# Attention tiles in shared rings, packed transposed weights, a larger landing reserve and a 128-row g_pre in a hybrid streaming encoder layer

## The chip, the cores and the metric

The kernel runs on one NeuronCore of a Trainium2 chip, on its five engines: TensorE (PE) multiplies, VectorE (DVE), ScalarE (ACT) and GpSimd (POOL) do the elementwise work, SyncE (SP) issues the DMAs. The metric is the device time of one execution in microseconds, and the lower the better.

## What is computed

One layer for a prompt of 1024 tokens and a later chunk of 32 tokens that share the weights; D = 1024, eight heads of 64 in each of two attention groups, float32 throughout. The reference, cut to what matters:

```python
def in_proj(h, g_pre, w_in):
    u = rmsnorm(h, g_pre) @ w_in                      # 1024 -> 4096
    qa, ka, va, ga, qb, kb, vb, gb = jnp.split(u, SPLIT_IDX, axis=-1)
def band_attention(q, k, v, q_pos, k_pos, bias_table):      # group A: softmax, own chunk and 8 before
    s = jnp.einsum('bqhd,bkhd->bhqk', q, k) * ATTN_SCALE + bias_table[:, rel][None]
    w = jax.nn.softmax(jnp.where(ok[None, None], s, NEG_INF), axis=-1)
    return jnp.einsum('bhqk,bkhd->bqhd', w, v)
def stick_breaking(q, k, v, q_pos, k_pos):                  # group B: strictly causal
    z = jnp.einsum('bqhd,bkhd->bhqk', q, k) * ATTN_SCALE
    log_beta = jax.nn.log_sigmoid(z)
    log_1m = jnp.where(causal, jax.nn.log_sigmoid(-z), 0.0)
    after = lax.cumsum(log_1m, axis=3, reverse=True) - log_1m
    w = jnp.where(causal, jnp.exp(log_beta + after), 0.0)
    return jnp.einsum('bhqk,bkhd->bqhd', w, v)
def finish(h, oa, ga, ob, gb, w_out, g_post, p, w_ple, w_ple_gate):
    y = jnp.concatenate([oa * jax.nn.silu(ga), ob * jax.nn.silu(gb)], axis=-1) @ w_out
    h = h + rmsnorm(y, g_post)
    return h + jax.nn.sigmoid(h @ w_ple_gate) * (p @ w_ple)
```

The sample chunk attends over a cache of 512 tokens and itself. New keys and values are outputs too.

## The kernel before

Every float32 product is made from two rounded parts: x = hi + lo, and PE adds hi*hi, hi*lo and lo*hi. So each operand is cast to hi by ACT or POOL, and lo = x - hi is made by DVE or POOL.

The work has three stages. **The start** loads x in nine tiles of 128 tokens (`load_x`, tiles x0 to x8, x3 and x4 in the tile x34), squares them on ACT (`scale_x`, tile sq), scales them with the row factor rs and with g_pre, transposes them on PE (`turn_x`, ptx) and keeps them as hnh and hnl in three chunks of 352 tokens. g_pre is spread to all partitions by a product of a column of ones with the row ghl (gpre). Beside this, half of p @ w_ple is made (tiles wph, wpl, php; results ple). Twelve matmuls on zeros (idle) stand ahead of everything on PE.

**The attention** takes eight pairs of heads, A0, B0, A1, B1 and so on to B3. `col_steps` projects a pair's k, q and v (mm_kA, mm_qA, mm_vA, 24 matmuls of 352 columns for each of three chunks); the weights of the next projection are loaded as wr and split into wh and wl (`ensure`). Keys and values go out, and the values are brought to token order through DRAM: DVE transposes 32x32 blocks (vx), a DMA writes swapA or swapB, four DMAs read it back into st (`values_out`), ACT copies it to vt, and `prep_v` splits it into v2. `prep_k` makes kd and kl with two copying DMAs, `prep_q` makes L.

For each head and each block i of 128 queries, `attention` has three steps. `scores(i)` makes S in PSUM from L, kd and kl, and the weights in two SBUF tiles of 1024 columns: w0 (named om) and w1 (named be). Group A adds the bias and takes the maximum on DVE, the exponential on ACT, the scaling by 1/sum on POOL. Group B takes two sigmoids on ACT, a scan on DVE and a product on POOL. `weights_t(i)` transposes w1 by blocks on PE into PSUM (ptw), and ACT and DVE evict it as hi and lo into wTh and wTl. `values(g)` multiplies four query blocks at once with v2 into PSUM (PV), 24 matmuls a head. om and be have three buffers each, wTh and wTl two each, of 4 x 512 columns: one for each group of four key blocks. The sample's heads run through the same tiles (`sample_attention`); its new values wait in vsT until then.

Projections of the next pair are woven between the attention steps as filling work for PE, and the gate projections (mm_gA, mm_gB) between and behind the last. Beside this POOL subtracts blocks of w_out and w_ple_gate (oB, gB) for the third stage.

**The finish** makes the output projection and the gate as seven block products in place of eight (o0P to g3P), and everything behind.

What sets the order of the instructions is a planner (`Recorder.order`, line 307). All steps are recorded first, each with its engine, an estimated duration and what it depends on. The planner then plays the program through: each engine takes, of what is ready at its time, the step with the lowest key, attention ahead of projections on PE. The result is written out as it stands, so each engine works strictly in that order. For a DMA it reckons the time at which it has landed:

```python
                line = max(line, t + o.busy + DMA_NS) + o.late
                done = line + DMA_MARGIN
```

DMA_NS is 1500 and DMA_MARGIN 800 (line 165). A tile's buffer comes free for the planner when the last use of the tile that held it has been placed. All instructions of the program are issued at line 385, so the profile names that line for all of them, and tiles tell them apart.

Of the kernel before, what the change touches and what calls it, by code (L numbers as in the profile page):

```python
# [13 lines left out]
P = 128  # L14
# [12 lines left out]
NT = 9  # L27

# [127 lines left out]

class Op:
# [7 lines left out]
DMA_NS, DMA_RATE, DMA_MARGIN = 1500, 320.0, 800  # L165
# [3 lines left out]
class Pool:  # L169
# [8 lines left out]
    def tile(self, shape, dtype, tag=None, name=None, bufs=1):  # L178
# [7 lines left out]
        line.append(b)  # L186
        return b
# [12 lines left out]
class Recorder:  # L200
# [43 lines left out]
    def add(self, eng, what, args, kw):  # L244
        writes, reads = [], []
        method = what[1] if isinstance(what, tuple) else ""
        for i, a in enumerate(args):
            if isinstance(a, (View, Raw)):
                (writes if i == 0 or (method == "tensor_tensor_reduce" and i == 7) else reads).append(a)
        for k, a in kw.items():  # L250
            if isinstance(a, (View, Raw)):
                (writes if k in ("out", "accum_out") else reads).append(a)
# [16 lines left out]
        if eng == "DVE":  # L269
            sbuf = [v for v in reads if isinstance(v, View) and not v.buf.psum and v.free() > 4]  # L270
# [3 lines left out]
    def cost(eng, method, args, kw, writes, reads):  # L274
# [3 lines left out]
        psum = any(isinstance(v, View) and v.buf.psum for v in reads)  # L278
# [96 lines left out]
    def emit(self, tc):  # L375
        ops = self.order()
        with tc.manual_schedule():
            for o in ops:
# [3 lines left out]
                args = [a.get() if isinstance(a, (View, Raw)) else a for a in o.args]  # L382
                kw = {k: a.get() if isinstance(a, (View, Raw)) else a for k, a in o.kw.items()}
# [7 lines left out]
def stream_step(  # L391
# [26 lines left out]
    r_dr = scratch([8, 768], "r_dr")  # L418
    ple_dr = scratch([T, D], "ple_dr")
# [55 lines left out]
    def ensure(j):  # L475
# [6 lines left out]
        if j == 2:  # L482
            pair = [at.tile([P, 2, 4, P], F32R, tag=tag, name=f"{tag}_{kind}{p}", bufs=2) for tag in ("wTh", "wTl")]
# [14 lines left out]
    def load_x(t):  # L498
        n = min(P, T - t * P)
        if t == 3:  # L500
            x34.append(at.tile([P, 2, D], F32, tag="wTh", name="x34", bufs=2))
        xt = x34[0][:, t - 3] if t in (3, 4) else at.tile([P, D], F32, tag="om", name=f"x{t}", bufs=3)
# [9 lines left out]
    def scale_x(t, xt, n, gp):  # L512
        sq = at.tile([P, D], F32, tag="be", name=f"sq{t}", bufs=3)
# [25 lines left out]
    def bias_rows():  # L539

        rb = at.tile([8, 257], F32, tag="om", name="rb", bufs=3)
        dma(rb, rel_bias[0])
        R = at.tile([8, 768], F32, tag="be", name="R", bufs=3)
# [101 lines left out]
    def col_steps(j):  # L645
# [65 lines left out]
    def attention(ab, p, h):  # L711
# [16 lines left out]
        def scores(i):  # L728
# [5 lines left out]
            w0 = at.tile([P, SEQ + 1], F32, tag="om", name=f"om{nm}_{i}", bufs=3)  # L734
            w1 = at.tile([P, SEQ], F32, tag="be", name=f"be{nm}_{i}", bufs=3)
# [31 lines left out]
            state[i] = w1  # L767

        wT = {}

        def weights_t(i):
            g, q = i // 4, (i % 4) * P
            for j in range(i // 4 + 1):
                if (g, j) not in wT:
                    wT[g, j] = [at.tile([P, 4, 4 * P], F32R, tag=tag, name=f"{tag}{nm}_{g}_{j}", bufs=2) for tag in ("wTh", "wTl")]
            b0 = lo_block(i)
            w1 = state.pop(i)
            b = b0
            while b <= i:
                j = b // 4  # L780
                e = min(i + 1, 4 * (j + 1))
                m = e - b
                pt = psum("T", f"ptw{nm}_{i}_{j}")
                for x in range(m):
                    nc.tensor.transpose(pt[:, x * P:(x + 1) * P], w1[:, (b - b0 + x) * P:(b - b0 + x + 1) * P], ident)
                hi, lo = wT[g, j]
                o = b - 4 * j
                src = pt[:, 0:m * P].rearrange("p (b c) -> p b c", b=m)
                nc.scalar.copy(hi[:, o:o + m, q:q + P], src)
                nc.vector.tensor_tensor(lo[:, o:o + m, q:q + P], src, f(hi[:, o:o + m, q:q + P]), ALU.subtract)  # L790
                b = e
# [946 lines left out]
```

## Time and profile before

| | |
|---|---|
| time, median of three runs | 824.11 us (823.62 to 825.51) |
| the profiled execution, its own time | 822.94 us |
| its span, first to last instruction | 821.2 us |
| PE busy | 806.5 us, 98% |
| DVE, ACT, POOL busy | 588.7, 536.5, 498.6 us |
| mean granted PE clock | 0.999 |
| DMA | 135.57 MB in 137855 packets |

A page of the profile and the views of its trace tell of one execution. Matmuls are pipelined and their ends are modelled, so the mean duration of a matmul holds the overlap with the next; the distance from one start to the next tells what a matmul costs. In a row of the timeline stand the start, the length that the instructions of the row cover together, the engine, the operation with out<-in, the count, and in brackets the idle time of the engine ahead of it with what ended it. In the list of waits a row names who waited for whom, the total in microseconds, how often, and the longest.

### The profile page before, as it was taken

Reading aid. Unit: us, or ns where it says so; the run is one execution under the profiler, and the core shown is the slowest. Engines: PE = TensorE matmul, PEld = TensorE weight load, DVE = VectorE, ACT = ScalarE, POOL = GpSimd, SP = SyncE. Lnnn points to the kernel's source line nnn. Section 1 sums busy time; section 2 is a strip of 40 time slices with the busy share of each in tenths; the row PEclk is TensorE's granted clock in tenths of the full one; section 3 lists DMA queues with packets and bytes.
Section 4 is the critical chain, followed back from the end, with each engine's and each line's share of the span. In section 5 each row is a group of like instructions: output and inputs, shape, how many; then the busy total and the mean of one; then the engine's idle time right before and its main releaser. Section 6 shows DMA issues by size and latency. Waiting matters only on the chain.

```text
span 821.2 us, 14722 instructions
## 1 busy us (share of the span) xinstructions
PE 806.5 (98%) x4814; PEld 742.7 (90%) x4814; DVE 588.7 (72%) x1165; ACT 536.5 (65%) x1179; POOL 498.6 (61%) x559
## 2 busy tenths in 40 slices
PE   9999999999999999999999999999999999999997
PEld 7999999999999998999999998999998787888786
DVE  5717588987687898687887787983664676686755
ACT  4735588776476667687685676653437866886741
POOL 5625785996676959554753454675462527599613
PEclk9999999999999999999999999999999999999999
DMA  8419854526764545633413544253489847749733
GB/s 296 122 39 277 208 178 149 142 60 203 214 178 155 152 135 153 154 91 88 97 40 98 139 122 145 74 160 112 134 264 291 293 142 242 252 153 361 248 117 128
DMA packets 137855, 135.57 MB, mean 165 GB/s; under 512 B 36450, under 2 KB 103818, under 8 KB 137779
## 3 DMA queue, kind: packets, MB, share of 16 engines
q1 hardware_dynamic: 137778, 134.64, 55.0%
q8 instruction: 38, 0.62, 0.3%
q14 instruction: 39, 0.31, 0.2%
HBM read 85.41 MB, written 40.79 MB: 154 GB/s over the span
## 4 chain that ended last, share of the span: by engine, by line
PE 83%; DVE 6%; ACT 4%; DMA 4%; issue 2%; SPq 0%; POOL 0%; DVEq 0%; ACTq 0%
PE mm_gB L385 5%; PE mm_qA L385 5%; PE mm_kB L385 5%; PE mm_kA L385 5%; PE mm_vA L385 4%; PE mm_vB L385 4%; PE mm_qB L385 4%; PE PVB L385 4%; PE SB L385 3%; PE ple L385 3%; PE PVA L385 3%; PE mm_gA L385 3%; PE ptwB L385 3%; PE ptwA L385 3%; PE SA L385 3%; PE g1P L385 2%
## 5 line engine op out<-in xcount | busy, mean ns | idle before, releaser
L385 POOL TENSOR_TENSOR beB<-beB,omB 128x128 f32<-128x128 f32 (+7 forms) x64 | 87.2, 1364 | 75.3 <-ACT beB L385 31.5
L385 DVE TENSOR_TENSOR_SCAN omB<-omB 128x128 f32<-128x128 f32 (+7 forms) x64 | 106.5, 1675 | 6.6 <-POOL omB L385 3.5
L385 POOL TENSOR_SCALAR beA<-beA,statA 128x640 f32<-128x640 f32 (+2 forms) x64 | 48.2, 755 | 50.1 <-DVE statA L385 47.9
L385 DVE TENSOR_TENSOR wTlA<-ptwA,wThA 128x128 fp32r<-128x128 f32 (+3 forms) x96 | 45.5, 483 | 27.8 <-ACT wThA L385 27.0
L385 ACT CAST wThA<-ptwA 128x128 fp32r<-128x128 f32 (+3 forms) x96 | 39.7, 422 | 32.1 <-PE ptwA L385 30.5
L385 ACT ACTIVATE omB<-SB 128x384 f32<-128x384 f32 (+5 forms) x96 | 47.1, 501 | 14.7 <-DVE SB L385 8.3
L385 DVE TENSOR_TENSOR wTlB<-ptwB,wThB 128x512 fp32r<-128x512 f32 (+3 forms) x96 | 50.7, 545 | 8.1 <-ACT wThB L385 7.2
L385 ACT CAST wThB<-ptwB 128x512 fp32r<-128x512 f32 (+3 forms) x96 | 44.7, 485 | 16.9 <-PE ptwB L385 16.3
L385 ACT ACTIVATE beA<-omA,statA 128x640 f32<-128x640 f32 (+2 forms) x64 | 44.7, 700 | 7.2 <-DVE statA L385 5.6
L385 ACT ACTIVATE beB<-SB 128x384 f32<-128x384 f32 (+5 forms) x96 | 45.4, 500 | 6.0 <-PE ptwB L385 3.2
L385 PE MATMUL ptwB<-ident,beB 128*128 128x128 f32 x288 | 44.9, 274 | 0.1
L385 PE MATMUL ptwA<-ident,beA 128*128 128x128 f32 x240 | 40.2, 274 | 0.8 <-POOL beA L385 0.8
L385 PEld LDWEIGHTS ptwB<-ident,beB 128*128 128x128 f32 x288 | 34.9, 140 | 3.4 <-DVE wTlB L385 0.8
L385 POOL TENSOR_TENSOR gB<-gB,gB 128x256 f32<-128x256 f32 x32 | 29.1, 929 | 13.8 <-issue 7.4
L385 PE MATMUL SB<-kdB,LB 128*128 128x384 f32 (+5 forms) x96 | 34.6, 364 | 0.3 <-ACT beB L385 0.2
L385 POOL TENSOR_TENSOR oB<-oB,oB 128x256 f32<-128x256 f32 x32 | 28.4, 903 | 8.6 <-DMA oB<-in_w_out_dram 4.6
L385 PE MATMUL SB<-klB,LB 128*128 128x384 f32 (+5 forms) x96 | 33.1, 346 | 0.0
L385 DVE CUSTOM_DVE_ANT_0 omA<-SA,biasA 128x320 f32<-128x320 f32 (+2 forms) x64 | 30.7, 479 | 3.2 <-PE SA L385 1.9
L385 PEld LDWEIGHTS ptwA<-ident,beA 128*128 128x128 f32 x240 | 30.2, 140 | 2.7 <-POOL beA L385 1.1
L385 PE MATMUL SA<-kdA,LA 128*128 128x320 f32 (+2 forms) x96 | 30.5, 327 | 1.4 <-DVE LA L385 1.2
L385 PE MATMUL SA<-klA,LA 128*128 128x320 f32 (+2 forms) x96 | 29.9, 321 | 0.0
L385 POOL TENSOR_TENSOR h<-h,x 128x512 f32<-128x512 f32 (+1 forms) x18 | 23.3, 1321 | 0.8 <-DVE h L385 0.8
(712 smaller groups left out, 2674.5 us busy)
## 6 DMA issues: line engine op xcount, KB each, us to landing
x<-in_x_prompt_dram SPq DMA_DIRECT2D x8, 512.0 KB, 5.9
oB<-in_w_out_dram SPq DMA_DIRECT2D x16, 256.0 KB, 4.0
sum_dro<-oB SPq DMA_DIRECT2D x16, 256.0 KB, 2.3
gB<-in_w_ple_gate_dram SPq DMA_DIRECT2D x16, 256.0 KB, 3.8
sum_drg<-gB SPq DMA_DIRECT2D x16, 256.0 KB, 2.8
x<-in_x_prompt_dram SPq DMA_DIRECT2D x16, 256.0 KB, 3.7
h_dr<-h SPq DMA_DIRECT2D x8, 512.0 KB, 3.5
ht<-h_dr SPq DMA_DIRECT2D x8, 512.0 KB, 5.5
```

The source lines that it names most:

```text
L385: getattr(getattr(tc.nc, o.what[0]), o.what[1])(*args, **kw)
```

## The change

It has five parts.

1. om and be are no longer buffers of 1024 columns but stretches of one long tile each (`Arena`): 3076 columns for om, 3384 for be. A tile takes the columns that it needs, one behind the other, and starts again at 0 where the rest is too short. It depends on the earlier tiles with which its columns overlap. All tiles that lived in om and be (x, sq, the bias rows, the sample's caches Kc and Vc) take their stretch there. In the changed kernel's order all of them are called om or be.
2. wTh and wTl become two such rings of 33 blocks of 128 columns. A group of four query blocks takes 13 or 20 blocks in A, 13 or 29 in B (`LAID`): the blocks of one query block lie side by side, and each query block starts 3, 4 or 7 blocks behind the one before. `weights_t` transposes four blocks at a time from the first on, and evicts them into one run; before, the cuts lay at multiples of four key blocks. `values` reads its moving operand as runs of 128 columns with a fixed step (`Segments`).
3. DMA_MARGIN goes from 800 to 2000.
4. g_pre: ones and ghl have 128 rows in place of one. Rows 1 to 127 of ghl are set to zero by two memsets on DVE.
5. The sample's new values go to DRAM (vs_dr) by a DMA for each pair, and come back into one tile vn for four heads; the POOL copies into vsT go.

The function `swapped` returns False for everything, so the branch behind it is never recorded. The diff, cut to its core:

```diff
-DMA_NS, DMA_RATE, DMA_MARGIN = 1500, 320.0, 800
+DMA_NS, DMA_RATE, DMA_MARGIN = 1500, 320.0, 2000
+class Segments:
+    def __init__(self, buf, start, step, n):
+        self.buf, self.start, self.step, self.n = buf, start, step, n
+        self.shape = [buf.shape[0], n, P]
+        self.box = (buf.box[0], (start, start + (n - 1) * step + P))
+    def get(self):
+        base = self.buf.get()[:, self.start:self.start + P]
+        return bass.AP(tensor=base.tensor, offset=base.offset, ap=[base.ap[0], [self.step, self.n], [1, P]])
+class Arena:
+    def tile(self, shape, name, dtype=None):
...
+        size = -(-n // 8) * 8
+        if self.at + size > self.cols:
+            self.at = 0
+        lo, hi = self.at, self.at + size
+        self.at = hi
...
+        for c, d, x in self.live:
+            if c < hi and lo < d:
+                old.append(x)
+                left += [(p, q, x) for p, q in ((c, lo), (hi, d)) if p < q]
+            else:
+                left.append((c, d, x))
...
-    vsT = const.tile([NS, 4, P], F32, tag="vsT", name="vsT")
+    ring0, ring1 = Arena(rec, at, "om", 3076), Arena(rec, at, "be", 3384)
+    ringh, ringl = (Arena(rec, at, x, 33 * P, F32R) for x in ("wTh", "wTl"))
...
-            nc.gpsimd.tensor_scalar(vsT[:, slot(ab, p), :], tok[0:NS, 8, :], 1.0, 1.0, ALU.mult, ALU.mult)
+            dma(vs_dr[ab][:, p * P:(p + 1) * P], tok[0:NS, 8, :])
...
-            w0 = at.tile([P, SEQ + 1], F32, tag="om", name=f"om{nm}_{i}", bufs=3)
-            w1 = at.tile([P, SEQ], F32, tag="be", name=f"be{nm}_{i}", bufs=3)
+            w0 = ring0.tile([P, n + (ab == "B")], f"om{nm}_{i}")
+            w1 = ring1.tile([P, n], f"be{nm}_{i}")
...
+        LAID = {("A", 0): (3, 13), ("A", 1): (4, 20), ("B", 0): (3, 13), ("B", 1): (7, 29)}
         def weights_t(i):
...
-                nc.scalar.copy(hi[:, o:o + m, q:q + P], src)
-                nc.vector.tensor_tensor(lo[:, o:o + m, q:q + P], src, f(hi[:, o:o + m, q:q + P]), ALU.subtract)
+            for b in range(0, n, 4):
+                m = min(4, n - b)
+                pt = psum("T", f"ptw{nm}_{i}_{b}")
                 for x in range(m):
+                    nc.tensor.transpose(pt[:, x * P:(x + 1) * P], w1[:, (b + x) * P:(b + x + 1) * P], ident)
+                c = slice(b * P, (b + m) * P)
+                nc.scalar.copy(hi[:, c], pt[:, 0:m * P])
+                nc.vector.tensor_tensor(lo[:, c], pt[:, 0:m * P], f(hi[:, c]), ALU.subtract)
...
-                nc.tensor.matmul(acc[:, c], v2[:, b, :], wT[g, j][half][:, b - 4 * j, c], start=(n == 0), stop=(n == len(todo) - 1))
+                step = LAID[ab, g][0]
+                w = Segments(wT[g][half], c.start * step + b * P, step * P, (c.stop - c.start) // P)
+                nc.tensor.matmul(acc[:, c], v2[:, b, :], w, start=(n == 0), stop=(n == len(todo) - 1))
...
+            vn = at.tile([NS, 256], F32, tag="ot", name="vn" + nm, bufs=3)
+            dma(vn, vs_dr[ab][:, 256 * gi:256 * gi + 256])
...
-    ones = at.tile([1, P], F32R, tag="ot", name="ones", bufs=3)
+    ones = at.tile([P, P], F32R, tag="ot", name="ones", bufs=3)
     nc.gpsimd.memset(f(ones), 1.0)
-    ghl = at.tile([1, 2, D], F32R, tag="wTl", name="ghl", bufs=2)
+    ghl = ringl.tile([P, 2, D], "ghl")
+    for part in range(2):
+        nc.vector.memset(f(ghl[:, part]), 0.0)
```

**What moves, at three places.** The first is PE's order just ahead of the first values product of pair B3 (PVB30), which waits for v2B30; SB30 are scores of the same head, ptksB1 a transpose for the sample, mm_gA0 the gate projection that fills. Before:

```order
L385 MATMUL ptksB10_6937<-ident_111,KcsB1_6841 128x128 x4
L385 MATMUL mm_gA0_1_6780<-hnh1_106,wl_gA0_1_6504 128x352
L385 MATMUL mm_gA0_1_6780<-hnl1_109,wh_gA0_0_6535 128x352 x2
L385 MATMUL ptksB11_6952<-ident_111,KcsB1_6841 128x128 x4
L385 MATMUL mm_gA0_1_6780<-hnl1_109,wh_gA0_0_6535 128x352 x2
L385 MATMUL mm_gA0_1_6780<-hnl1_109,wh_gA0_1_6566 128x352 x4
L385 MATMUL mm_gA0_2_6915<-hnh2_107,wh_gA0_0_6535 128x352 x3
L385 MATMUL PVB30_0_6872<-wThB30_0_0_6805,v2B30_6408 128x512
```

Now, in the same place:

```order
L453 MATMUL SB30_7_0_6602<-kdB30_5743,LB30_5749 128x512
L453 MATMUL SB30_7_0_6602<-klB30_5748,LB30_5749 128x512
L453 MATMUL mm_gA0_1_6452<-hnh1_108,wl_gA0_1_6169 128x352 x4
L453 MATMUL mm_gA0_1_6452<-hnl1_111,wh_gA0_0_6184 128x352 x2
L453 MATMUL SB30_7_1_6619<-kdB30_5743,LB30_5749 128x512
L453 MATMUL SB30_7_1_6619<-klB30_5748,LB30_5749 128x512
L453 MATMUL mm_gA0_1_6452<-hnl1_111,wh_gA0_0_6184 128x352 x2
L453 MATMUL ptwB30_4_0_6628<-ident_113,be_147 128x128 x4
L453 MATMUL mm_gA0_1_6452<-hnl1_111,wh_gA0_1_6239 128x352 x4
L453 MATMUL mm_gA0_2_6570<-hnh2_109,wh_gA0_0_6184 128x352 x4
L453 MATMUL mm_gA0_2_6570<-hnh2_109,wh_gA0_1_6239 128x352 x3
L453 MATMUL PVB30_0_6522<-wTh_493,v2B30_6096 128x512
```

The scores of block 7 and the transposes of block 4 have moved ahead of this product, and the gate projections follow behind them.

The second is ACT's order around the casts of pair B1's value weights (wh_vB1, which wait for the DMA into wr_vB1), in head A10. Before:

```order
L385 CAST wThA10_1_1_2800<-ptwA10_6_1_2930 128x3x128
L385 CAST wThA10_1_0_2522<-ptwA10_7_0_2931 128x128
L385 CAST wh_vB1_0_2778<-wr_vB1_0_2909 128x512
L385 ACTIVATE stqB1_2478<-mm_qB1_1_2807 128x352
L385 CAST wh_vB1_1_2785<-wr_vB1_1_2910 128x512
L385 CAST wThA10_1_1_2800<-ptwA10_7_1_2982 128x4x128
```

Now:

```order
L453 ACTIVATE stqB1_2296<-mm_qB1_1_2718 128x352
L453 CAST wTh_493<-ptwA10_6_4_2825 128x128
L453 ACTIVATE be_147,statA11_2_2544<-om_133,statA11_2_2544 128x384
L453 CAST wTh_493<-ptwA10_7_0_2826 128x512
L453 CAST wh_vB1_0_2697<-wr_vB1_0_2782 128x512
L453 CAST wh_vB1_1_2709<-wr_vB1_1_2783 128x512
L453 CAST wTh_493<-ptwA10_7_4_2858 128x128
```

A projection's eviction and an exponential now stand ahead of the two casts, and of the transposed weights one block stands behind them, before four.

The third is POOL's order in head A01: the rows be with stat are the scalings that the transposes on PE wait for, oB the differences of w_out blocks that wait for loads. Before:

```order
L385 TENSOR_SCALAR beA01_0_1228<-beA01_0_1228,statA01_0_994 128x128
L385 TENSOR_TENSOR oB110_974<-oB220_973,oB110_974 128x256
L385 TENSOR_TENSOR oB210_1235<-oB110_974,oB210_1235 128x256 x2
L385 TENSOR_SCALAR beA01_1_1315<-beA01_1_1315,statA01_1_1012 128x256
L385 TENSOR_TENSOR wl_kA1_0_1307<-wr_kA1_0_865,wh_kA1_0_1328 128x512
```

Now:

```order
L453 TENSOR_SCALAR be_147<-be_147,statA01_0_974 128x128
L453 TENSOR_SCALAR be_147<-be_147,statA01_1_987 128x256
L453 TENSOR_TENSOR oB120_922<-oB120_922,oB110_924 128x256 x2
L453 TENSOR_TENSOR oB110_924<-oB220_923,oB110_924 128x256
L453 TENSOR_SCALAR be_147<-be_147,statA01_2_1007 128x384
```

The scaling of block 1 has moved ahead of the differences, and the differences come later in the head.

More of the change, by code (lines that the diff above doesn't have):

```diff
@@ L27, with swapped @@
 NT = 9
+def swapped(ab, p, h, i):
+    return False
 LAG_T = 2
@@ L277, in cost @@
         n = out.free() if isinstance(out, View) else 1
-        psum = any(isinstance(v, View) and v.buf.psum for v in reads)
+        psum = any(isinstance(v, (View, Segments)) and v.buf.psum for v in reads)
         if eng == "PE":
@@ L482, in ensure @@
         if j == 2:
-            pair = [at.tile([P, 2, 4, P], F32R, tag=tag, name=f"{tag}_{kind}{p}", bufs=2) for tag in ("wTh", "wTl")]
+            pair = [ringl.tile([P, 2, 4, P], f"w{x}_{kind}{p}") for x in "hl"]
         for kh in range(2):
@@ L766, in scores @@
                 nc.gpsimd.tensor_scalar(w1[:, 0:n], w1[:, 0:n], m[:, 3:4], 1.0, ALU.mult, ALU.mult)
-            state[i] = w1
+            state[i] = w0, w1
         wT = {}
+        LAID = {("A", 0): (3, 13), ("A", 1): (4, 20), ("B", 0): (3, 13), ("B", 1): (7, 29)}
         def weights_t(i):
[L772 to L775, printed above, removed]
+            g = i // 4
+            step, size = LAID[ab, g]
+            if g not in wT:
+                wT[g] = [x.tile([P, size * P], f"{x.name}{nm}_{g}") for x in (ringh, ringl)]
```

97 lines of the change are left out of this document (64 added, 33 removed).

## The prediction, made before the changed kernel had run

> **What bounds the kernel now.** I read the page first: the shares of the engines and the chain that ended last.
>
> ```profile
> PE 806.5 (98%) x4814; PEld 742.7 (90%) x4814; DVE 588.7 (72%) x1165; ACT 536.5 (65%) x1179; POOL 498.6 (61%) x559
> PE 83%; DVE 6%; ACT 4%; DMA 4%; issue 2%; SPq 0%; POOL 0%; DVEq 0%; ACTq 0%
> ```
>
> TensorE (PE) is the bound, and the change leaves it the same 4814 matmuls of the same widths. So a gain can only come from PE standing idle or running slowly. The table of busy time by stretches tells where it stands idle; the columns are the stretch, its length, then the busy time of each engine.
>
> ```profile
> 20.00:25.00 5.00, 4.32 (x28) 3.62 (x27) 3.25 (x7) 4.36 (x12) 4.59 (x8) 1.00 0.96 316
> 40.00:62.00 22.00, 22.00 (x142) 21.38 (x141) 4.13 (x9) 7.34 (x15) 4.79 (x9) 1.00 0.16 42
> 62.00:130.00 68.00, 65.32 (x426) 62.84 (x425) 47.90 (x131) 46.51 (x108) 47.09 (x60) 1.00 0.75 202
> 200.00:270.00 70.00, 68.19 (x451) 65.74 (x450) 51.68 (x132) 47.05 (x111) 46.70 (x63) 1.00 0.64 184
> 480.00:545.00 65.00, 62.94 (x405) 59.84 (x404) 54.87 (x85) 44.74 (x99) 40.55 (x43) 1.00 0.48 139
> 780.00:821.20 41.20, 36.43 (x169) 29.96 (x168) 21.58 (x35) 13.26 (x23) 10.31 (x8) 0.98 0.38 122
> ```
>
> Of 14.7 us idle, 4.8 are the tail, which the change leaves alone, and 6.6 lie in three stretches of the attention (2.7, 1.8 and 2.1). The waits of PE name them:
>
> ```profile
> PE PVB L385 <- DVE v2B L385: 1.8, 1, 1.8
> PE PVA L385 <- ACT wThA L385: 1.2, 1, 1.2
> PE SA L385 <- DVE LA L385: 1.2, 1, 1.2
> PE ptwA L385 <- POOL beA L385: 0.8, 1, 0.8
> PE PVA L385 <- DVE v2A L385: 0.6, 1, 0.6
> PE ptksB L385 <- DVE v2B L385: 0.5, 1, 0.5
> ```
>
> All but the third go back to a DMA that landed later than the order had reckoned. The timeline shows the engine that stood before such a landing, with its idle time and releaser in brackets:
>
> ```profile
> 510.21 1.05 ACT L385 COPY vtB<-stvB 128x1024 f32<-128x1024 f32 x1 [2.95 <-DMA stvB<-swapB]
> 221.71 0.62 ACT L385 CAST wh_vB<-wr_vB 128x512 fp32r<-128x512 f32 x1 [2.90 <-DMA wr_vB<-in_w_in_dram]
> 105.67 0.73 POOL L385 TENSOR_TENSOR oB<-oB,oB 128x256 f32<-128x256 f32 x1 [2.05 <-DMA oB<-in_w_out_dram]
> ```
>
> ACT waits for the swapped values at 510, and the values product waits behind it (1.8 us). At 221 it waits for raw weights, with the last cast of the transposed weights queued behind (1.2). At 105 POOL waits for w_out, with a softmax scaling queued behind (0.8). Together 4.9 us of PE time hang on landings.
>
> The other slow place is the start, PE's timeline:
>
> ```profile
> 1.31 2.93 PE L385 MATMUL idle<-newh 128*128 128x256 f32 x12 [1.31 <-DVE newh L385]
> 4.05 1.94 PE L385 MATMUL ptp<-ident,pp 128*128 128x128 f32 x8
> 5.92 2.07 PE L385 MATMUL gpre<-ghl,ones 1*128 1x512 f32 x4
> 7.92 3.78 PE L385 MATMUL ple<-wph0True,php 128*128 128x512 f32 x8
> 11.50 1.91 PE L385 MATMUL ple<-wpl0True,php 128*128 128x512 f32 x4
> 13.21 2.37 PE L385 MATMUL ple<-wph1True,php 128*128 128x512 f32 x8
> 15.42 0.60 PE L385 MATMUL ptx<-ident,sq 128*128 128x128 f32 x4
> 34.68 3.90 PE mm_vA L385 x24
> 625.11 5.57 PE ple L385 x24
> ```
>
> The last two rows, from the chain, give full speed: 162 ns for 352 columns, 232 ns for 512. From 11.50 to 13.21 four 512-column matmuls took 427 ns each: half speed. The next eight took 2.21 us, which is two at 427 and six at 232, so the speed doubled near 14.0 us, 6.1 us after the first matmul with 128 rows of real data (7.92). The granted clock reads 1.00 all this time, so that column does not show it.
>
> **The change part by part.**
>
> *Landings get 1.2 us more reserve.* This moves instructions and costs none. Between the last projection of a pair's values and the first product that reads them, PE must have enough other work. I counted it in both orders: columns at 0.461 ns (3.90 us / 24 / 352), transposes at 0.10 us (eight in 0.82 us, next rows).
>
> ```profile
> 265.35 1.06 PE L385 MATMUL ptksB<-ident,KcsB 128*128 128x128 f32 x8 [0.52 <-DVE v2B L385]
> 266.17 0.83 PE L385 MATMUL PVB<-wThB,v2B 128*128 128x512 f32 x4
> ```
>
> Pair B3: 26,784 columns and 24 transposes before (14.7 us), 29,856 and 28 now (16.6): +1.8, its whole wait of 1.8. A0: 42,144 and 20 to 45,312 and 23, +1.8 against a wait of 0.6. B1: 29,600 and 31 to 32,768 and 23, +0.7 against 0.5. But B2 goes from 35,072 and 19 to 33,088 and 15, to 16.8 us. Work plus wait was 16.5 us in B3 and 17.2 in B1, so that is what such a chain needs, and B2, B3 and B0 (33,792 and 15, 17.1) now stand at that edge. I leave 0.5 us of waits there (0 to 1.2). Of 2.9 us this saves 2.4.
>
> The cast that waited at 221 now stands 1.0 us of PE work behind its DMA's issue, where it stood 0.0, but the last cast of the transposed weights is still queued behind it. Of 1.2 us 0.2 stay: 1.0 saved (0 to 1.2). On POOL the w_out difference stands 0.9 us behind its issue, before 0.0, and one more scaling ahead of it: 0.6 of 0.8 saved (0 to 0.8).
>
> The reserve brings one new short stretch: between pair B0's last q projection and its first scores stood 21,440 columns and 19 transposes, now 6,784 and 5 (3.6 us). A0 had 8,448 and 1 (4.0 us) and waited 1.2 for LA; B2 (7,136 and 5) and B3 (7,488 and 5) had no such wait. I take 0.4 (0 to 1.2).
>
> *g_pre by 128 rows.* The four gpre matmuls cost the same. If their rows are what counts as work, the 6.1 us run from 5.92 instead of 7.92: 2.0 us at half speed turn into 1.0, and I take 0.9, since part may be lost in waits behind it. The end on one side is 0. On the other it counts from 1.31, when PE began, and the next limit is the first normalized tile:
>
> ```profile
> 11.82 2.94 DVE L385 SCALAR_TENSOR_TENSOR sq<-x,rs,gpre 128x512 f32<-128x512 f32 x4 [2.44 <-POOL rs L385]
> 0.87 0.38 DVE L385 MEMSET newh<- 128x384 f32 x1 [0.87 <-PEq L1726]
> 2.18 0.81 DVE L385 CAST ghl<-grow 1x1024 fp32r<-1x1024 f32 x1 [0.93 <-DMA grow<-in_g_pre_dram]
> 3.02 1.21 DVE L385 TENSOR_TENSOR ghl<-grow,ghl 1x1024 fp32r<-1x1024 f32 x1
> 5.79 0.69 DVE L385 TENSOR_TENSOR php<-ptp,php 128x512 fp32r<-128x512 f32 x1 [1.55 <-ACT php L385]
> ```
>
> Its first half is there at 12.6, its transposes begin at 15.42, so at most 2.8. What PE gains here it mostly keeps: from 40 to 62 us it has no idle time to swallow it. The two new memsets of 1024 columns cost VectorE about 1.0 us each by the 384-column row; ghl then ends near 5.3 (1.25 + 2.0 + 0.81 + 1.21), gpre starts at 5.92, and the cover is 0.6 us thick. Without it each 0.1 us more would delay PE by as much. [...]
>
> *Two rings by width, packed weights.* The rings take the size that a tile has, so more tiles fit at once; the transposes keep their number, and each row of weights is cut into four blocks and the rest. The evictions now write one run; the contiguous php above took 0.69 us for 512 columns, as did a cast with gaps:
>
> ```profile
> 223.72 0.69 DVE L385 TENSOR_TENSOR wTlA<-ptwA,wThA 128x512 fp32r<-128x512 f32 x1 [3.86 <-ACT wThA L385]
> L385 PE MATMUL PVB<-wThB,v2B x96: 221/365/501, 141.7 to 590.6; 128*128 128x512 f32 x48, 128*128 128x384 f32 x16, 128*128 128x256 f32 x16, 128*128 128x128 f32 x16
> ```
>
> So nothing there. A ring of 33 blocks holds only one of B's groups (13 and 29 blocks), so group 1's first cast waits for group 0's product; the order knows this, and it costs nothing while projections fill PE. The values products now read their moving operand in runs of 128 columns. No row shows PE doing that. It cannot gain. The upper bound is the fixed part of a matmul at each new run: 232 ns = a + 512 b and 162 = a + 352 b give a = 8 ns. The row above has (48 x 3 + 16 x 2 + 16) = 192 such joints; low halves double it, A has 288: 672 joints, 5.4 us. I take 0, because a row of evictions with gaps costs nothing extra.
>
> *Sample values through DRAM.* Eight small POOL operations go and twelve DMAs come; POOL is not the bound:
>
> ```profile
> L385 POOL TENSOR_SCALAR vsT<-vtA x4: 287/287/318, 76.5 to 443.7; 32x128 f32<-32x128 f32 x4
> ```
>
> They are due tens of us before use; POOL's 2.3 us in all lie beside PE's work. 0, and if the cover is gone, one landing of some 3 us, as at 510.
>
> **Sum.** -2.4 - 1.0 - 0.6 + 0.4 - 0.9 = -4.5. The order is drawn anew for the whole attention, and what I have not counted will bring some waits of its own; the waits that stay in the list above come to 1.2, and I add half, 0.6: **-3.9**. The profiled execution took 822.94 (span 821.2), so 819.0 for such a one; the median of the three runs lies 1.17 above it, so I forecast 824.11 - 3.9 = **820.2**.
>
> **The rivals.**
>
> 1. *The start gains all, no wait is left.* -2.8 and -4.9: 816.4. For it: the counted stretches grew by as much as the waits. Against it: two shrank. Chance 0.09.
> 2. *Rows do not count.* Whatever holds the clock back until 14.0 is then the same now: half speed ends where it did, the start term is 0, and 824.11 - 3.0 = 821.1. For it: the eight transposes from 4.05 on use all 128 rows and did not help either. Against it: the one-row matmuls are what stands right before the 6.1 us. Chance 0.20. [...]
> 3. *The reserve only moves waits.* An order with 98% PE has no room; each pushed-back step makes PE meet another late one, in B2, B0 or a place not counted, and the start gains nothing. Saved 4.0, new 4 or so: 822.6 to 825. For it: the new short q stretch. Chance 0.17.
> 4. *Slower: the run joints cost.* At 8 ns each the 672 joints cost 5.4 us in the values products, all on PE's path: 820.2 + 5.4 = 825.6. It decides from 3.9 us / 672 = 6 ns a joint; beyond that the change loses. For it: no row shows such a read. Against it: the evictions with gaps. [...] Chance 0.06.
> 5. *The change does not do what it says:* one head's tiles collide in a ring. The waits on each engine's list number about the same in both orders (PE 749 before, 754 now); 0.02, somewhat slower.
>
> The forecast itself has 0.46. A difference under 0.2% (1.6 us) can hardly be told from no change here. Faster by more than that (under 822.5): 0.46 + 0.09 + 0.20 = 0.75; within: 0.17; slower: 0.08. The range, 816.8 to 823.6, takes the forecast with the ends of the start, the waits and the redrawing, reaches most of rival 1 and a part of rival 3, holds rival 2, and leaves out rivals 4 and 5.
>
> **What would show it.** Right: the ple matmuls at half speed end 1 to 3 us earlier; PE's waits for v2, wTh and be lose most of their 4.9 us; the 512-column values products keep their mean of about 0.41 us. Wrong: half speed still to 14 us; new PE waits of 1 us and more from 62 to 545, first at LB near 110; values products longer by 10 ns and more.

## The result and the profile after

The changed kernel took 815.1 us (median of 7 runs, 814.4 to 818.4), the kernel before in the same rounds 823.6 (7 runs, 819.7 to 826.2): a ratio of 0.991, 95% interval 0.9887 to 0.9934. That is 8.5 us less where 3.9 were forecast, and it lies below the range. In the later rounds the kernel before took 821.9 to 822.7 (medians of 19 to 28 runs), so part of the 8.5 can be the draw of these seven runs; in those rounds the changed kernel with g_pre by one row stood 6.6 us below it. The profiled execution took 815.1 with a span of 813.3.

The page of the changed kernel, the engines' shares and the chain that ended last:

```profile
PE 800.3 (98%) x4814; PEld 739.0 (91%) x4814; DVE 576.3 (71%) x1159; ACT 536.8 (66%) x1179; POOL 495.9 (61%) x551
PE 89%; ACT 4%; DMA 2%; POOL 2%; DVE 1%; issue 1%; SPq 0%; POOLq 0%
```

PE's part of the chain rose from 83 to 89%, DVE's fell from 6 to 1, DMA's from 4 to 2. The busy time by stretches (stretch, length, then PE, PEld, DVE, ACT, POOL):

```profile
62.00:130.00 68.00, 66.81 (x439) 64.85 (x438) 52.49 (x137) 50.18 (x119) 49.08 (x60) 1.00 0.67 189
200.00:270.00 70.00, 69.17 (x458) 66.81 (x457) 57.97 (x124) 46.81 (x108) 49.87 (x63) 1.00 0.59 167
480.00:545.00 65.00, 64.32 (x413) 61.69 (x412) 52.29 (x77) 43.29 (x96) 43.80 (x42) 1.00 0.47 137
```

PE's idle time in the three stretches fell from 2.7, 1.8 and 2.1 us to 1.2, 0.8 and 0.7. In the first, DVE did 52.5 us of work against 47.9, ACT 50.2 against 46.5, which fits a softmax that is made earlier. What PE still waits for:

```profile
PE ptx L453 <- DVE be L453: 1.7, 2, 0.9
PE SA L453 <- DVE LA L453: 1.1, 1, 1.1
PE SB L453 <- ACT be L453: 0.8, 2, 0.5
PE PVB L453 <- DVE v2B L453: 0.7, 1, 0.7
PE ptwB L453 <- DVE OsB L453: 0.7, 1, 0.7
PE mm_kB L453 <- ACT stvA L453: 0.5, 1, 0.5
PE PVA L453 <- ACT wTh L453: 0.3, 1, 0.3
```

The landings (v2, wTh, and be through POOL) stand here with 1.0 us, before with 4.9. The two places on ACT at which it stood 2.95 and 2.90 us for a landing, now (the second wait is spread over two casts, 2.2 us together, with one cast of transposed weights behind them):

```profile
505.37 1.05 ACT L453 COPY vtB<-stvB 128x1024 f32<-128x1024 f32 x1 [1.45 <-DMA stvB<-swapB]
216.90 0.62 ACT L453 CAST wh_vB<-wr_vB 128x512 fp32r<-128x512 f32 x1 [1.11 <-DMA wr_vB<-in_w_in_dram]
218.66 0.62 ACT L453 CAST wh_vB<-wr_vB 128x512 fp32r<-128x512 f32 x1 [1.13 <-DMA wr_vB<-in_w_in_dram]
```

And the start:

```profile
1.30 2.93 PE L453 MATMUL idle<-newh 128*128 128x256 f32 x12 [1.30 <-DVE newh L453]
4.04 1.37 PE L453 MATMUL ptp<-ident,pp 128*128 128x128 f32 x8
5.16 1.19 PE L453 MATMUL gpre<-wTl,ones 128*128 128x512 f32 x4
6.66 2.10 PE L453 MATMUL ple<-wph0True,php 128*128 128x512 f32 x8 [0.31 <-ACT wph0True L453]
12.42 0.66 PE L453 MATMUL ptx<-ident,be 128*128 128x128 f32 x4 [0.94 <-DVE be L453]
```

Here full speed came within the eight transposes from 4.04 (1.37 us, before 1.94), ahead of g_pre's matmuls; so g_pre cannot have brought it. And of the 9 us that this is earlier, PE waits part away, since be is there only at 12.42.

Put together from PE's first starts in the two traces: pair A0's key transposes (ptkA) came 1.6 us earlier, from there to the first output projection (o0P) 565.6 us passed in place of 572.3, and 0.4 came back in the finish: -1.6 - 6.7 + 0.4 = -7.9, the spans' difference. To see where the 6.7 came from I took, for each PE instruction of that stretch, the time to the next one's start, less the median of its width (161 ns for 352 columns, 232 for 512, 108 for a transpose). Steps of over 0.6 us lost 7.2 us in 6 places before and 4.3 in 5 after; steps of 0.1 to 0.6 us lost 5.7 us in 30 places before and 2.8 in 17 after; the rest 7.2 and 6.3. The forecast spoke almost only of the first kind. The values products with 512 columns:

```profile
L453 PE MATMUL PVB<-wTl,v2B 128*128 128x512 f32 x48 | 15.8, 410 | 0.0
L453 PE MATMUL PVB<-wTh,v2B 128*128 128x512 f32 x48 | 15.4, 399 | 0.7 <-DVE v2B L453 0.7
```

### The profile page after: what moved, and what is told of

Same layout as the page of the kernel before. It is cut to its first block, busy times and chain, and to the rows that moved or that the text cites. A ratio compares the mean times of both kernels' runs of the same rounds, so it can differ in the third digit from the quotient of the medians.

```text
span 813.3 us, 14716 instructions
## 1 busy us (share of the span) xinstructions
PE 800.3 (98%) x4814; PEld 739.0 (91%) x4814; DVE 576.3 (71%) x1159; ACT 536.8 (66%) x1179; POOL 495.9 (61%) x551
## 4 chain that ended last, share of the span: by engine, by line
PE 89%; ACT 4%; DMA 2%; POOL 2%; DVE 1%; issue 1%; SPq 0%; POOLq 0%
PE mm_gB L453 6%; PE mm_kB L453 6%; PE mm_qA L453 5%; PE mm_qB L453 5%; PE mm_kA L453 5%; PE mm_gA L453 5%; PE mm_vA L453 5%; PE PVB L453 4%; PE mm_vB L453 4%; PE SB L453 4%; PE ptwB L453 4%; PE SA L453 3%; PE PVA L453 3%; PE ptwA L453 3%; PE g0P L453 2%; PE g1P L453 2%
## 5 line engine op out<-in xcount | busy, mean ns | idle before, releaser
L453 POOL TENSOR_TENSOR be<-be,om 128x128 f32<-128x128 f32 (+8 forms) x66 | 90.5, 1379 | 67.9 <-DVE om L453 27.4
L453 DVE TENSOR_TENSOR_SCAN om<-om 128x512 f32<-128x512 f32 (+8 forms) x66 | 102.3, 1562 | 8.1 <-ACT om L453 7.8
L453 POOL TENSOR_SCALAR be<-be,statA 128x640 f32<-128x640 f32 (+2 forms) x64 | 42.6, 670 | 45.2 <-DVE statA L453 34.0
L453 ACT CAST wTh<-ptwB 128x512 fp32r<-128x512 f32 (+3 forms) x96 | 44.3, 483 | 25.3 <-PE ptwB L453 24.0
L453 DVE TENSOR_TENSOR wTl<-ptwB,wTh 128x512 fp32r<-128x512 f32 (+3 forms) x96 | 50.0, 545 | 14.0 <-ACT wTh L453 13.6
L453 DVE TENSOR_TENSOR wTl<-ptwA,wTh 128x512 fp32r<-128x512 f32 (+2 forms) x96 | 44.8, 482 | 16.4 <-ACT wTh L453 15.6
L453 ACT ACTIVATE om<-SB 128x384 f32<-128x384 f32 (+5 forms) x96 | 47.5, 499 | 11.7 <-DVE SB L453 9.2
L453 ACT ACTIVATE be<-om,statA 128x640 f32<-128x640 f32 (+2 forms) x64 | 44.7, 700 | 10.5 <-DVE statA L453 7.8
L453 ACT ACTIVATE be<-SB 128x384 f32<-128x384 f32 (+5 forms) x96 | 45.5, 506 | 4.5 <-DVE Vl2sB L453 1.5
L453 PE MATMUL ptwB<-ident,be 128*128 128x128 f32 x288 | 44.0, 273 | 0.7 <-DVE OsB L453 0.7
```

The costliest lines, as they stand in the source:

```text
L453: getattr(getattr(tc.nc, o.what[0]), o.what[1])(*args, **kw)
```

## The experiments

Theory at the outset (R): the gain in the attention comes from the landings' reserve. Rivals: G, the rings give room; C against N at the start, whether the rows of a matmul count for the clock or only that PE is issued to; later L, that any redrawn order comes out better or worse by luck.

**One part alone, or one part undone.** Reserve alone, on the kernel before:

```diff
-DMA_NS, DMA_RATE, DMA_MARGIN = 1500, 320.0, 800
+DMA_NS, DMA_RATE, DMA_MARGIN = 1500, 320.0, 2000
```

> The kernel before with the landings' reserve alone: 800 to 2000 ns, no rings, g_pre by one row. Theory R (nearly the whole gain in the attention comes from landings that the order now sets early enough): from the first key transposes of pair A0 to the first output projection the time falls from 572.3 us by 5 us or more, and the run takes about 5 us less than the kernel before of the same rounds. Rival G (the rings let the order move more work, the reserve alone gives only what I had counted): 2 to 4 us less, and the other half shows in the kernel with rings alone. The start: like before, half speed to about 14 us in the profile.

Measured 818.45 against 821.96 (ratio 0.9943, 0.9923 to 0.9962): 3.5 us less, the stretch from ptkA to o0P 569.3 us. That is G's figure. Its longest waits in the attention:

```profile
PE mm_kB L385 <- ACT stvA L385: 1.5, 1, 1.5
PE SA L385 <- DVE LA L385: 1.0, 1, 1.0
PE ptwB L385 <- DVE wTlB L385: 1.0, 1, 1.0
PE SB L385 <- ACT beB L385: 0.8, 2, 0.6
```

No wait for v2, wTh or be through POOL is left, as forecast, but three new ones of 1.5, 1.0 and 0.8 stand in their place.

g_pre by 128 rows alone, on the kernel before:

```diff
-    ones = at.tile([1, P], F32R, tag="ot", name="ones", bufs=3)
+    ones = at.tile([P, P], F32R, tag="ot", name="ones", bufs=3)
-    ghl = at.tile([1, 2, D], F32R, tag="wTl", name="ghl", bufs=2)
+    ghl = at.tile([P, 2, D], F32R, tag="wTl", name="ghl", bufs=2)
+    for part in range(2):
+        nc.vector.memset(f(ghl[:, part]), 0.0)
```

> The kernel before with g_pre by 128 rows alone. Theory C (the rows of the matmuls count for the clock, so full speed comes earlier, or surely instead of by luck): the profile has the ple matmuls of the start at full speed by 8 us or so instead of 14, the time falls by 1.5 to 3 us, and the runs lie in one group, where those of before lie in two about 4 us apart (819.7 to 820.7 and 823.6 to 826.2). [...]

Measured 821.59 against 821.96 (0.9993, 0.9974 to 1.0011): no difference that can be told, as N would have it, where C had said 1.5 to 3 us. Its profile, one of the slower of its runs (823.5), shows another thing, at the same cast on ACT as at 221 before. The stretches at it, and PE's timeline:

```profile
220.00:225.00 5.00, 3.04 (x13) 2.78 (x13) 1.98 (x8) 2.86 (x8) 3.21 (x5) 0.74 0.58 199
225.00:230.00 5.00, 5.00 (x35) 4.92 (x34) 4.13 (x13) 2.11 (x7) 1.07 (x1) 0.92 0.43 95
```

```profile
222.07 1.20 PE L385 MATMUL PVA<-wThA,v2A 128*128 128x512 f32 x4 [1.96 <-ACT wThA L385]
224.53 1.07 PE L385 MATMUL ptwsA<-ident,w1sA 128*128 128x128 f32 x4
```

PE waited 1.96 us, and the granted clock (the column behind POOL's) fell to 0.74 and 0.92: four transposes took 1.07 us, in the trace of before 0.61 (ptwsA, from 225.24). The wait was 0.8 us longer than in the trace of before; PE's starts fell back by 2.3 us against that trace, so the slow clock cost about 1.5 more. (A wait of 2.5 us near 265 for a DMA, where PE had waited 0.5 before, took another 1.9, and PE had been 2.4 us ahead until 221. So this one execution tells nothing of the median.)

The rings, the packed weights and the sample values alone (the changed kernel with both edits above undone):

```diff
-DMA_NS, DMA_RATE, DMA_MARGIN = 1500, 320.0, 2000
+DMA_NS, DMA_RATE, DMA_MARGIN = 1500, 320.0, 800
-    ghl = ringl.tile([P, 2, D], "ghl")
+    ghl = ringl.tile([1, 2, D], "ghl")
```

> The changed kernel with the reserve back at 800 ns and g_pre by one row: of the change only the rings, the packed weights and the sample values through DRAM are left. Theory R: within 1.5 us of the kernel before. Rival G: 2 to 4 us less than before. Rival J (joints between runs of 128 columns cost up to 8 ns): slower by up to 5 us, and the 512-column values products gain 10 ns or more in mean.

Measured 817.67 (0.9949, 0.9928 to 0.9970): 4.3 us less by the part that I had put at 0, a little more than G's 2 to 4. Theory R falls, and so does J.

The changed kernel with g_pre by one row:

> The changed kernel with g_pre back at one row, everything else as changed. Theory C: 1.5 to 3 us slower than the changed kernel (815.1), so 816.6 to 818, with runs in two groups and half speed to about 14 us in some of them. Rival N: 815.1 within 0.8 us, in the same groups as the changed kernel.

Measured 815.33 (0.9917, 0.9893 to 0.9941), 0.2 us over the changed kernel's median, 0.6 by the ratios to the kernel before: N's figure; but two of its six runs took 817.1 and 817.7, the others 814.2 to 815.6.

**Which half of the rings.** Score rings alone (om and be; weights in the old blocks), then packed weights alone (om and be in fixed buffers). The edits, of the changed kernel with reserve 800 and one row:

```diff
-            pair = [ringl.tile([P, 2, 4, P], f"w{x}_{kind}{p}") for x in "hl"]
+            pair = [at.tile([P, 2, 4, P], F32R, tag=tag, name=f"{tag}_{kind}{p}", bufs=2) for tag in ("wTh", "wTl")]
...
-            w0 = ring0.tile([P, n + (ab == "B")], f"om{nm}_{i}")
-            w1 = ring1.tile([P, n], f"be{nm}_{i}")
+            w0 = at.tile([P, SEQ + 1], F32, tag="om", name=f"om{nm}_{i}", bufs=3)
+            w1 = at.tile([P, SEQ], F32, tag="be", name=f"be{nm}_{i}", bufs=3)
```

The first two lines with `weights_t` and `values` of the kernel before make the former; the last four, and the like for the other om and be tiles, the latter.

> Of the change only the two rings for scores (om, be) and the sample values through DRAM; weights in the old blocks of 16, reserve 800, g_pre one row. Rings, packing and sample values together took 4.3 us off the kernel before, where I had put 0. Theory S (room for scores: more softmax rows fit at once, so PE meets fewer late ones): 3 us or more of the 4.3 are here, 818 to 819 against a kernel before near 822. Rival P (packed weights give it): within 1 us of the kernel before. Rival L (it is neither; any redrawn order comes out 2 us better or worse): this and the kernel with packed weights alone both land anywhere between 818 and 824, and their gains don't add to 4.3.

> Of the change only the packed weights in their two rings and the sample values through DRAM; scores in three fixed buffers each, reserve 800, g_pre one row. Theory S: within 1.3 us of the kernel before. Rival P: 3 us or more under it. Rival L: as said for the kernel with the score rings alone.

Measured 821.76 (1.0003, 0.9989 to 1.0017) and 821.11 (0.9986, 0.9973 to 0.9999). Neither half gives the 4.3 us at this reserve; S and P both miss, L seemed to hold. The profile of the score rings shows two long waits that go against their gain. The first, in ACT's and PE's timeline and the stretches:

```profile
466.06 0.62 ACT L453 CAST wh_vB<-wr_vB 128x512 fp32r<-128x512 f32 x1 [4.74 <-DMA wr_vB<-in_w_in_dram]
466.58 0.47 ACT L453 CAST wThA<-ptwA 128x384 fp32r<-128x384 f32 x1
467.70 1.12 PE L453 MATMUL ptwA<-ident,be 128*128 128x128 f32 x4 [2.62 <-DVE wTlA L453]
```

```profile
465.00:470.00 5.00, 2.38 (x10) 2.21 (x10) 2.91 (x9) 3.79 (x10) 3.24 (x3) 0.73 0.39 114
470.00:475.00 5.00, 5.00 (x34) 4.80 (x34) 3.38 (x14) 2.61 (x9) 0.98 (x5) 0.93 0.05 12
```

It is the landing of raw weights with a cast of transposed weights queued behind it again: 2.6 us of PE, and half speed afterwards (granted clock 0.73 and 0.93; four transposes in 1.12 us, four at 472.32 in 0.61). A second one (2.8 us) stands near 219, where the kernel before waited 1.2. With the same rings and a larger reserve (1400 and 2500 ns, below) PE's waits for these casts come to 0.4 us and to none.

**More draws of the order.** The same kernels with other reserves; each edit is the one number.

> The changed kernel with 3000 ns of reserve instead of 2000. If the reserve helps because the landings are late by up to some 2 us, 3000 takes away what is left of such waits (0.7 before the values products at 507 us): 814 to 815.5. Rival (the reserve only has a best value, and beyond it the order spends its work too early): 816 to 819. Rival L: anywhere within 2 us of 815.

> The kernel before with 3000 ns of reserve, nothing else. At 2000 it was 3.5 us faster than the kernel before (818.45 to 821.96). If what counts is that landings get enough, 3000 is within 1 us of that. Rival (a best value near 2000): 820 to 822. Rival L: anywhere from 816 to 822.

Measured 816.91 (0.9941, 0.9929 to 0.9953) with rings and 817.71 (0.9957, 0.9935 to 0.9979) without: the first as the rival had it, the second within 1 us of 2000.

> The kernel before with 1400 ns of reserve. So far: 800 gave 821.9, 2000 818.5, 3000 817.7. Theory M (with the old buffers the time falls as the reserve grows, since landings come up to 2 us later than reckoned, and each redrawing of the order adds or takes 1 to 2 us by chance): 818 to 821. Rival F (the reserve has nothing to do with it, 800 is just an unlucky draw): as good as 2000 and 3000, 817 to 819.

> The changed kernel with 1400 ns of reserve. So far, with rings: 800 gave 817.7, 2000 815.2, 3000 816.9. Theory Q (the two rings together give room that is worth 2 to 4 us under any reserve): 815 to 818, and under the kernel before with 1400 by 2 us or more. Rival L (the 4.3 us of the rings at 800 were a lucky draw): no steady gap to the kernel before with the same reserve; it can be slower.

> The kernel before with 2500 ns of reserve. Theory M: 816.5 to 819.5, near 818. Rival F: 817 to 822, anywhere.

> The changed kernel with 2500 ns of reserve. Theory Q: 814.5 to 817.5, under the kernel before with 2500 by 1 us or more. Rival L: no steady gap. With it there are five draws with rings and five without.

Measured without rings 821.86 at 1400 (0.9985, 0.9963 to 1.0007) and 822.46 at 2500 (1.0000, 0.9983 to 1.0018): M falls, for there is no trend. With rings 813.08 (0.9881, 0.9852 to 0.9911) and 811.84 (0.9864, 0.9830 to 0.9899), better than Q had said. L becomes unlikely: the gap has one sign at all five reserves, which luck alone would bring in one case of 16.

> Only the score rings (and the sample values through DRAM), weights in the old blocks of 16, reserve 2500. Theory B (both kinds of room are needed: as long as one of them is full the other's freedom only moves the waits): 819 to 823, as without rings (822.5). Theory S (the score rings give most of it, and 821.8 at 800 was an unlucky draw): 813 to 817. Rival P (the packed weights give it): 819 to 823.

> Only the packed weights (and the sample values through DRAM), scores in three fixed buffers each, reserve 2500. Theory B: 819 to 823. Theory S: 819 to 823. Rival P: 813 to 817.

> As the kernel with score rings alone, reserve 1400. Without rings 821.9, with both 813.1. Theory B: 818.5 to 823. Theory S: 813 to 817. Rival P: 818.5 to 823.

> As the kernel with packed weights alone, reserve 1400. Theory B and theory S: 818.5 to 823. Rival P: 813 to 817. If score rings and packed weights each stand some 2 to 4 us below the kernel before in the mean over the three reserves, both halves give a part and the parts add; that would end theory B.

Measured, score rings alone: 815.82 (0.9936, 0.9914 to 0.9959) and 818.00 (0.9948, 0.9929 to 0.9968); packed weights alone: 820.34 (0.9974, 0.9953 to 0.9994) and 821.33 (0.9994, 0.9974 to 1.0014). Theory S, which had missed at 800, holds at 2500 and nearly at 1400; P falls; B falls as an all-or-nothing. All medians in us, by reserve in ns:

| | 800 | 1400 | 2000 | 2500 | 3000 |
|---|---|---|---|---|---|
| buffers of before | 821.9 | 821.9 | 818.5 | 822.5 | 817.7 |
| packed weights alone | 821.1 | 821.3 | | 820.3 | |
| score rings alone | 821.8 | 818.0 | | 815.8 | |
| both (the change's) | 817.7 | 813.1 | 815.1 | 811.8 | 816.9 |

Taken as ratios to the kernel before of the same rounds, the gaps between the last row and the first are 0.5, 1.0, 0.3, 1.4 and 0.2%: 0.68% in the mean, 5.6 us, with a standard error of 1.9 (95% interval 0.4 to 10.8). The kernels of the last row have g_pre by 128 rows except at 800, all others by one row, so four of the five gaps hold what g_pre gives; alone it moved the medians by 0.2 to 0.4. Within a row the reserve makes no trend, but the draws spread by a standard deviation of 2.1 us (first row) and 3.0 (last). At 800, 1400 and 2500 the mean gains are 2.7 us for the score rings, 0.8 for the packed weights, 8.0 for both, each with an error of some 2 by this spread: neither half by itself is clear of noise. Whether both together give more than the sum is open: 4.5 us more, with an error of some 2.7.

What the room does can be seen in the profile. The work on scores alone by stretches, group A then group B (first PE, with counts of matmuls in brackets), with the buffers of before at 2500:

```profile
62.00:95.00 33.00, 8.28 (x36) 5.95 (x36) 7.32 (x15) 1.00 0.93 247
100.00:130.00 30.00, 3.23 (x14) 2.09 (x14) 1.42 (x5) 4.78 (x12) 1.00 0.45 137
```

and with the score rings alone at 2500:

```profile
62.00:95.00 33.00, 10.60 (x46) 7.63 (x46) 11.12 (x22) 1.00 0.95 247
100.00:130.00 30.00, 5.62 (x22) 3.61 (x22) 1.85 (x7) 8.89 (x21) 1.00 0.38 114
```

Of pair A0's 48 score matmuls 46 have begun by 95 us, with the old buffers 36; of B0's 48 already 22 by 130, against 14. Part of this is the start, which was 1.9 us earlier in this execution. Counted from the first key transposes (ptkA), A0's last score matmul begins 27.7 to 33.5 us later in all eleven profiles with score rings, and 38.1 to 43.3 in all nine with fixed buffers, packed weights or not. So the room does let the softmax run ahead; that a narrow row of weights no longer holds a full buffer is the likely reason, read from the code.

Running ahead is not yet a gain: the kernel with score rings alone at 800 does it most (27.7) and took 821.76. What it saves is PE's waits. Counted as in the section on the result, from ptkA to o0P, in us, one execution each:

| | 800 | 1400 | 2000 | 2500 | 3000 | mean |
|---|---|---|---|---|---|---|
| steps over 0.6 us, buffers of before | 7.2 | 10.6 | 6.2 | 8.1 | 5.2 | 7.5 |
| steps over 0.6 us, both rings | 6.6 | 1.4 | 4.3 | 1.5 | 6.4 | 4.0 |
| steps of 0.1 to 0.6 us, buffers of before | 5.7 | 4.1 | 4.4 | 4.7 | 5.3 | 4.8 |
| steps of 0.1 to 0.6 us, both rings | 2.9 | 3.7 | 2.8 | 2.1 | 2.6 | 2.8 |

The short ones are fewer in every pair (20 to 33 against 12 to 19) and give 2.0 us; the long ones give more in the mean, 3.4, but not in every pair. With the score rings alone at 1400 and 2500 the short ones stay (5.5 and 4.7 us) and the long ones fall to 3.5 and 2.2. One long wait goes with the score buffers: near 310 PE waits for ACT's copy stvA, here in the kernel before at 3000:

```profile
310.40 1.54 PE L385 MATMUL mm_kB<-hnh,wh_kB 128*128 128x352 f32 x4 [3.02 <-ACT stvA L385]
```

At 1400 to 3000 this wait took 1.5 to 3.0 us with the buffers of before and 2.4 and 3.4 with packed weights alone, but at most 1.0 with score rings, alone or with the packed weights. At 800 it was 0.5 or less everywhere. Why ACT comes late there was not traced.

**The clock at the start.** The four g_pre matmuls issued eight times over, by one row and by 128:

```diff
-    for kh in range(2):
+    for kh in [0, 1] * 8:
```

> The changed kernel with g_pre by one row, and the four g_pre matmuls issued eight times over (32 of 512 columns: 14.7 us at half speed, 7.4 at full). Theory C (a one-row matmul does not count as work for the clock): wherever half speed stands when they begin, it stays, and if full speed had come before, it is lost again within the stretch; the ple matmuls behind them begin at 427 ns each. [...]

> The changed kernel (g_pre by 128 rows) with the four g_pre matmuls issued eight times over. [...] If half speed lasts as long as with one row, neither rows nor issue explain the start.

One row:

```profile
5.87 14.02 PE L453 MATMUL gpre<-wTl,ones 1*128 1x512 f32 x32
19.81 2.50 PE L453 MATMUL ple<-wph0True,php 128*128 128x512 f32 x5
25.57 1.98 PE L453 MATMUL ple<-wph1True,php 128*128 128x512 f32 x8
```

128 rows:

```profile
5.78 7.67 PE L453 MATMUL gpre<-wTl,ones 128*128 128x512 f32 x32
13.29 1.30 PE L453 MATMUL ple<-wph0True,php 128*128 128x512 f32 x5
```

With one row 14 us of busy PE did not bring full speed, 0.44 us a matmul, and it came some 4 us after the first ple matmul, which has 128 rows; with 128 rows, 127 of them zeros, the 32 took 0.24 us each. As to the clock theory C holds in these two runs: rows count. These are one execution each, of 825.7 and 818.3 us.

## Why the prediction was wrong

**The step that failed** is the term of the two rings and the packed weights, "So nothing there". I priced the instructions, found none that cost or gain, and gave the room no price, though the same paragraph says that more tiles fit at once. Measured, it is 4.3 us at a reserve of 800, and 5.6 in the mean of five reserves, which holds a little of g_pre. The score rings alone give 2.7 of the 8.0 us at three reserves, the packed weights 0.8, each with an error of some 2; the rest comes only with both, or is the draw of the order. It shows in waits that my list could not name: short ones of 0.1 to 0.6 us, and long ones that another order does not have.

**The reserve**, -3.6 with the new q stretch. As a list of waits this came out: 4.9 us at landings became 1.0, forecast 0.9. B0's new short q stretch, forecast at 0.4, costs nothing: no wait stands ahead of B0's first scores at 108.4 us. As a cause it did not come out. With the old buffers the reserve gave 0.2, 3.5, -0.4 and 4.2 us (1400 to 3000) and put other waits where the old ones went; there rival 3's mechanism was the right one. With both rings 1400 to 3000 are all faster than 800, by 0.8 to 5.8 us, without a trend; they have g_pre by 128 rows, 800 has not.

**g_pre**, -0.9. That rows count was right, as the long runs show (0.44 us a matmul by one row, 0.24 by 128); the path to a gain was not, and the size was too large. I let 6.1 us run from the first matmul that counts, with g_pre as that one. But the idle matmuls and the transposes ahead of it have 128 rows too. In seven profiles with g_pre by one row, five had full speed by 6.6 us (the rings alone, the changed kernel by one row, packed weights alone at 800, 1400 and 2500) and two, the kernel before and the reserve alone, only after 13.5 us. Two of the five lost it again. The changed kernel, g_pre by 128 rows alone and the long run by 128 rows had it by 8.0 us and kept it through the start; counts this small could be luck. ptkA came at 65.99 us in the kernel before and at 64.38 in the changed one: as an estimate, two times 1.6 us in seven make 0.5 on average; the medians moved by 0.4 and 0.2. The half speed to 14.0 that I took for the kernel's own looks like a draw: with the buffers of before, 14 matmuls began from 5 to 10 us at a reserve of 2000 and 21 at 3000. So the 9 us shown above are no gain of the change. Rival 2 priced this term rightly, by a mechanism that the long runs refute.

**The run joints**, 0, and rival 4: right. The 512-column products took 399 and 410 ns; in the same view before, 406 and 410:

```profile
L385 PE MATMUL PVB<-wThB,v2B 128*128 128x512 f32 x48 | 15.9, 406 | 1.9 <-DVE v2B L385 1.8
L385 PE MATMUL PVB<-wTlB,v2B 128*128 128x512 f32 x48 | 15.8, 410 | 0.2 <-DVE wTlB L385 0.2
```

**The redrawing**, +0.6: the sum wanted a spread, not a term. Orders that differ in one number lie 2 to 3 us apart, so even the right terms would not have carried a range of 3.4 us either way. Part of the 8.5 may be such a draw, and 2500 is a better one: the changed kernel with that reserve took 811.84 (0.9864 of the kernel before). The **sample values** by themselves were not tried; they are in the kernel with score rings at 800, which stands at 1.0003.

Rival 1's 816.4 came nearest, by luck: neither the start nor the listed waits gave what it had said.

## What to carry to other kernels

Price room as well as instructions: where a scheduler allots buffers, a tile of its own width instead of the widest lets the other engines run ahead, and what that saves is in waits that the list of one trace does not name. Before crediting one number in a planner, run three or four neighbours of it: here the neighbours lay further apart than the effect that was forecast. And before reading a slow start from one profile, look at several.

## What the runs showed of the hardware

One-row matmuls kept PE busy, but did not bring full speed: 32 of them took 14.02 us in the long run above. Also, full speed was lost within a few us. The kernel with packed weights alone at 800 had it when g_pre began at 5.27 us (four matmuls in 1.19), and then one-row matmuls and a wait of 1.84 us for ACT came together; PE's timeline and the stretches:

```profile
5.27 1.19 PE L453 MATMUL gpre<-wTl,ones 1*128 1x512 f32 x4
8.30 3.48 PE L453 MATMUL ple<-wph0True,php 128*128 128x512 f32 x8 [1.84 <-ACT wph0True L453]
11.62 1.07 PE L453 MATMUL ple<-wpl0True,php 128*128 128x512 f32 x4
```

```profile
6.00:8.00 2.00, 0.46 (x2) 0.02 (x1) 0.25 (x1) 0.37 (x1) 0.00 (x0) 0.97 0.94 297
8.00:10.00 2.00, 1.70 (x4) 1.41 (x5) 1.24 (x2) 1.35 (x4) 1.28 (x1) 0.50 1.00 374
10.00:12.00 2.00, 2.00 (x7) 1.59 (x7) 0.15 (x1) 1.89 (x3) 0.68 (x2) 0.68 1.04 403
```

The eight matmuls from 8.30 took 3.32 us to the next one's start, 0.42 each, with the granted clock at 0.50 and 0.68. With packed weights at 1400 the column reads 0.68 from 8 to 10 us, 0.50 from 10 to 12 and 0.98 from 12 to 15. The column of the granted clock shows such a loss, but not the half speed at the program's start: there it reads 1.00 in the kernel before until 14.0 us, with matmuls of 427 ns.

In the attention a PE wait cost more than its length, about 1.5 us more behind the 1.96 us in the kernel with g_pre by 128 rows alone. Half speed stood behind that wait, behind one of 2.62 us (score rings alone at 800) and one of 3.02 (the kernel before at 3000), and behind one of 2.0 at 315 in the kernel before at 2500 (granted clock 0.74). It did not follow another of 2.0 near 495 in that same execution, nor waits of 2.46 us (g_pre by 128 rows alone, near 265) and 2.77 (score rings alone at 800, near 219): the column reads 1.00 there. And with packed weights alone at 800 PE stood idle for only 1.22 us in all from 310 to 315, and the clock of the next 5 us was 0.66. So the length alone does not decide. Counted from the clock column (what is missing to 1.00, times the length of the stretch, times two), half speed lasted 3.4 us in five of these losses: with g_pre by 128 rows alone, with the score rings alone, with packed weights alone near 315, and in the two at the start. Behind the wait of 3.02 us it lasted 6.8:

```profile
305.00:310.00 5.00, 2.19 (x12) 1.45 (x10) 4.43 (x5) 4.90 (x10) 4.92 (x3) 0.92 0.71 181
310.00:315.00 5.00, 4.60 (x18) 4.44 (x19) 3.36 (x9) 2.33 (x6) 4.92 (x3) 0.50 0.20 41
315.00:320.00 5.00, 5.00 (x33) 4.98 (x32) 3.94 (x10) 2.43 (x7) 3.68 (x5) 0.90 0.47 135
```
